# Gate loads a tile ahead, latents written back over their own tile, and two sets of transposes emitted later, in a one-core hybrid encoder layer

## The chip, the core and the metric

The kernel runs on one core of a Trainium2 chip. The metric is the device time of one execution in microseconds (us); below, "the time" is the median of several runs. The engines are TensorE (PE, matmuls and transposes; its weight loads are shown as PEld), VectorE (DVE), ScalarE (ACT), GpSimd (POOL) and SyncE (SP), which issues most of the DMA transfers from its queue.

## The reference

One layer is computed for 1024 new frames of one stream (the prompt) and 64 frames of a running stream (the sample, with 512 cached frames); together 1088 tokens of width 1024.

- Both streams are normalised, scaled and shifted by a conditioning vector, and projected once: `proj = h @ w_in`.
- Group A is latent attention. `latent_new = rms_norm(c_kv, g_kv_lora)` (256 wide) is an output and also the source of keys and values: `kv = (latent @ w_ukv)`, 4 heads of 128 + 128; a rotary part of 64 is appended to each key, the key is RMS-normalised per head and rotated. Attention is block-causal in chunks of 64.
- Group B is a gated linear recurrence, 4 heads with a state of 64x128: `o, s_new = gla_recurrence(q, k, v, log_a, s0)`, then `rms_norm(o, g_gla_out) * silu(r)`, where `r` is a part of the projection.
- The two groups are concatenated, projected by `w_out`, gated and added to the input; a squared-ReLU MLP of width 4096 follows.

All is in float32. The kernel computes each product of two float32 operands as three passes over split operands (high x high, high x low, low x high).

## The kernel before

Tokens are held in nine tiles of 128 (the ninth, tile 8, has the 64 frames of the sample); some products run over three chunks of 384, 384 and 320 tokens. `mm3` (L91 to L95) issues the three matmuls of one product, so most PE time stands under the lines L93, L94 and L95.

The program is emitted by several generators at once. `interleave` (L46) is a small planner: each generator yields (PE time it has just emitted in ns, a waiting time in ns, a condition), and the planner always takes the first generator in its list that is due, and adds its PE time to a clock. If none is due, the clock jumps. So the numbers in the `yield` lines are costs and due times by which instructions are put in program order; they are no waits on the chip. On the chip each engine runs its instructions in one order, and waits where an operand or a buffer isn't there. The order on an engine is not in all places the order of the program: a scheduler puts an instruction ahead of earlier ones when it takes it for ready sooner.

The kernel has these stages; the change touches the second to the fourth.

1. To some 95 us: normalisation, the first projection columns.
2. About 95 to 275 us: `interleave([weights, gla(), main(), gates(), lats])`. `gla` (L655) is the recurrence, a tile at a time, with a hierarchy of 7 levels of halves (6 for the tile of 64), each level a pair of matmuls (L747) between ACT and DVE work (`prep`, L671; masked copies, L755). After the last level the output `o` of the tile is multiplied out (L790, L794), squared on ACT (L799), scaled on POOL and DVE (L802, into `og`), and a closure `tail` (L805) is kept: it transposes `og` on PE (L808), copies the result with the gain on ACT into `mog` (L811) and stores it to `mix_d` in DRAM (L812). That closure is called in the next tile, after level 3 (L784). `main` (L573) runs the projections of values and gates meanwhile and stores the swish input to `r_d` (L618).
3. `gates` (L820) starts when all of `r_d` and `mix_d` has been emitted. For each of the nine tiles it loads `r` (L825) and the recurrence's output `mx` (L826) into two tiles of a ring of four buffers called `gv`, yields 1000, applies Silu on ACT (L829), multiplies on DVE (L830) and stores (L831). Beside it `latents` (L620) computes the compressed latents: 24 matmuls (`rows`, L265, into a bank `mm`), the sum of squares on ACT (L628), the root on POOL (L120, L121), the scaling on DVE into `cn` (L630, two buffers), an output (L634, L637). One tile later its transposes follow (L644: two on PE into a bank `tp`, of which there are two), two copies on ACT into a tile `cl` of one buffer (L647) and a store to `lat_d` (L648).
4. About 300 to 400 us: `interleave([weights, past_keys(), lats, query_main(), query_latents()])`, and then to about 610 us the attention stage with `keys_stream`, `queries_stream` and three `worker`s. The keys and values of a tile are made in `keys_values` (L876), for the cached frames (`past_keys`, L1056, whose latents are transposed at L1066) and for the new ones (`new_keys`, L1078): two groups of 12 matmuls of 512 columns with copies to `kn` and sums of squares on ACT (L900), a root on POOL (L904, L905), two multiplications on DVE (L907 into `kn`, L908 into `krt`), then a yield of 4500, four transposes of `kn` on PE (L914) and, 800 later, four of `krt` (L921). `query_main` (L1221) is the other PE work of this stage: nine blocks of 24 matmuls.
5. From 610 us to the end: output projection and MLP.

The pools of stage 2 and 3 (`gw`, which holds `gv`, and others) are closed after `gates`, and the pools of stage 4 (`kw` of the keys, `qp` of the query columns) are opened in that memory; a new tile there waits for the last use of the old tile in its place.

Of the kernel before, what the change touches and what calls it, by code (L numbers as in the profile page):

```python
# [10 lines left out]
F32 = mybir.dt.float32  # L11
# [3 lines left out]
ALU = mybir.AluOpType  # L15
# [4 lines left out]
P = 128  # L20
# [10 lines left out]
TILES = [(i * P, P) for i in range(8)] + [(SEQ, DEC)]  # L31
# [40 lines left out]
def layer(ctx: ExitStack, tc: tile.TileContext, I, O):  # L72
    nc = tc.nc
    ACT, DVE, POOL, PE, SP = nc.scalar, nc.vector, nc.gpsimd, nc.tensor, nc.sync
# [10 lines left out]
    def tp_bank():  # L85
        return psT.tile([P, 512], F32, name="tp")

    def g_bank():
        return psG.tile([P, 512], F32, name="g")
# [7 lines left out]
    def heads(ap):  # L97
        return ap.rearrange("p (h t) -> p h t", h=H)
# [123 lines left out]
    def has(*keys):  # L222
        return lambda: all(k in done or k in groups for k in keys)
# [3 lines left out]
    dp = hctx.enter_context(tc.tile_pool(reuse_waits="tile", name="dp", bufs=2, side="right"))  # L227
# [37 lines left out]
    def rows(key, off, n, w):  # L265

        wh, wl = groups[key]
        ps = mm_bank()
        for kt in range(KT):
            mm3(ps[:n, :w], h["h"][:, kt, off:off + n], h["l"][:, kt, off:off + n], wh[:, kt, :w], wl[:, kt, :w],  # L270
                kt == 0, kt == KT - 1)
            yield w * 1.25, 0, None
        return ps[:n, :w]
# [261 lines left out]
    with gctx:  # L535
# [84 lines left out]
        def latents():  # L620
            yield 2000, 0, has("D1")
            for i in (8, 0, 1, 2, 3, 4, 5, 6, 7):
                off, n = TILES[i]
                s = i == 8
                ps = yield from rows("D1", off, n, 320)
                cn_ = dp.tile([P, 256], F32, name="cn")
                s2 = dp.tile([P, 2], F32, name="s2")
                ACT.activation(cn_[:n], ps[:, 0:256], AF.Square, accum_out=s2[:n, 0:1])  # L628
                rstd(s2[:n, 1:2], s2[:n, 0:1], n, 1, 1.0 / 256)
                DVE.tensor_scalar(out=cn_[:n], in0=ps[:, 0:256], scalar1=s2[:n, 1:2], scalar2=None, op0=ALU.mult)  # L630
                ki = 12 if s else i
                ACT.copy(kraw[:n, ki], ps[:, 256:320])
                lat = dp.tile([P, 256], F32, name="lat", bufs=1)
                DVE.tensor_tensor(out=lat[:n], in0=cn_[:n], in1=gkv_bc[:n], op=ALU.mult)  # L634
                ol, ok = (O["lat_s"], O["kr_s"]) if s else (O["lat_p"], O["kr_p"])
                oo = 0 if s else off
                ACT.dma_start(ol[oo:oo + n], lat[:n])  # L637
                SP.dma_start(ok[oo:oo + n], kraw[:n, ki])
                tails.append((i, off, n, cn_))
                while len(tails) > (0 if i == 7 else 1):  # L640
                    j, o2, n2, c2 = tails.pop(0)
                    tp = tp_bank()
                    for b in range(2):
                        PE.transpose(tp[:, b * P:b * P + n2], c2[:n2, b * P:(b + 1) * P], ident[:n2, :n2])  # L644
                    cl = dp.tile([P, 2, P], F32, name="cl", bufs=1)
                    for b in range(2):
                        ACT.activation(cl[:, b, :n2], tp[:, b * P:b * P + n2], AF.Copy, scale=gkvT[:, b:b + 1])  # L647
                    SP.dma_start(lat_d[:, :, o2:o2 + n2], cl[:, :, :n2])  # L648
                    done.add(f"lat {j}")
                    yield 220, 1500, None  # L650
            done.add("end D1")
# [3 lines left out]
        def gla():  # L655
            rot = 0
            tail = None
# [54 lines left out]
            for i, (off, n) in enumerate(TILES):  # L712
# [23 lines left out]
                for lv, hf in enumerate(halves):  # L736
                    (kl, ql), nb = ready.pop(0), n // (2 * hf)
                    if lv + 2 < len(halves):
                        ready.append(prep(halves[lv + 2]))
                    elif begun is None:  # L740
                        if i + 1 < len(TILES) and f"gates {i + 1}" in done:
                            begun = begin(i + 1)
                    else:
                        begun[5].append(begun[2](begun[4][1]))
                    sc = g_bank()[:, 0:2 * P].rearrange("p (c j t) -> p c j t", c=2, j=2)
                    for p in range(2):
                        PE.matmul(sc[:n, p, :, :n // 2], lhsT=kl[:, n * p:n * p + n], rhs=ql[:, :, p, :n // 2],  # L747
                                  start=True, stop=True)
                    sc = sc[:n, :, :, :n // 2].rearrange("p c j (b h) -> p (c j) b h", h=hf)
                    to = ST[:n, :, :n].rearrange("p c (b r h) -> p r c b h", r=2, h=hf)[:, 1]  # L750
                    if nb == 1:
                        ACT.copy(to[:hf], sc[:hf])
                    else:
                        mlv = 6 - (hf.bit_length() - 1)
                        DVE.copy_predicated(to, masks[:n, mlv, :n // 2].rearrange("p (o b h) -> p o b h", o=1, h=hf)  # L755
                                            .broadcast_to([n, H, nb, hf]), sc)
                    yield 440, 1800, None
                    if lv == 0:
                        tp = tp_bank()
                        for p in range(2):  # L760
                            PE.transpose(tp[:n, P * p:P * p + P], kk[:, p, :n], ident)
                        kt_ = gw.tile([P, 256], F32, name="kt_", bufs=1)
                        ACT.copy(kt_[:n], tp[:n, 0:256])
                    if lv == 2:
                        sp = g_bank()
                        for p in range(2):
                            PE.matmul(sp[:, 256 * p:256 * p + 256], lhsT=kt_[:n, P * p:P * p + P],
                                      rhs=gv[:n, 256 * p:256 * p + 256], start=True, stop=True)
                        for p in range(2):
                            for j in range(2):  # L770
                                ps, cs = slice(64 * j, 64 * j + 64), slice(P * j, P * j + P)
                                src = sp[ps, 256 * p + P * j:256 * p + P * j + P]
                                if i == 0:
                                    ACT.copy(sb_new[ps, p, cs], src)
                                else:
                                    DVE.scalar_tensor_tensor(out=sb_new[ps, p, cs], in0=sb_old[ps, p, cs],
                                                             scalar=E1[ps, p, n - 1:n], in1=src,
                                                             op0=ALU.mult, op1=ALU.add)
                        if i >= 7:
                            dst = O["st_s"] if smp else O["st_p"]  # L780
                            for p in range(2):
                                for j in range(2):
                                    SP.dma_start(dst[2 * p + j], sb_new[64 * j:64 * j + 64, p, P * j:P * j + P])
                    if lv == 3 and tail is not None:  # L784
                        tail()
                        tail = None
                o = mm_bank()
# [10 lines left out]
                for hd in range(H):  # L798
# [4 lines left out]
                                  in1=s4[:n, 4:8].rearrange("p (h t) -> p h t", t=1).broadcast_to([n, H, P]), op=ALU.mult)  # L803
# [16 lines left out]
        def gates():  # L820

            yield 0, 2000, has("end C1", "gla out")
            for i, (off, n) in enumerate(TILES):
                r, mx = (gw.tile([P, 512], F32, name="gv", bufs=4) for _ in range(2))
                SP.dma_start(heads(r)[:, :, :n], r_d[:, :, off:off + n])  # L825
                SP.dma_start(heads(mx)[:, :, :n], mix_d[:, 4:8, off:off + n])  # L826
                yield 0, 1000, None
                r, mx = (heads(t)[:, :, :n] for t in (r, mx))
                ACT.activation(r, r, AF.Silu)  # L829
                (DVE if i % 2 else DVE).tensor_tensor(out=r, in0=r, in1=mx, op=ALU.mult)  # L830
                SP.dma_start(mix_d[:, 4:8, off:off + n], r)  # L831

        lats = Stream(latents())
# [42 lines left out]
    def keys_values(lh, ll, ki, tab, n, kv, slot):  # L876
# [11 lines left out]
                          in1=t_[:n, :, 32:64].broadcast_to([n, 2, 32]), op=ALU.subtract)  # L888
        DVE.tensor_tensor(out=R[:n, 0, :, 32:64], in0=a[:n, :, 32:64].broadcast_to([n, 2, 32]),
                          in1=t_[:n, :, 0:32].broadcast_to([n, 2, 32]), op=ALU.add)  # L890
        kr = kw.tile([P, H, P], F32, name="krt", bufs=1)
        for g in range(2):
# [6 lines left out]
            for j in range(2):  # L899
# [8 lines left out]
        DVE.tensor_tensor(out=kr[:n], in0=R[:n].rearrange("p t d c -> p t (d c)").broadcast_to([n, H, P]),  # L908
                           in1=rs, op=ALU.mult)
        cs = slice(P * slot, P * slot + n)  # L910
        yield 0, 4500, None
        tp = heads(tp_bank())
        for hd in range(H):
            PE.transpose(tp[:, hd, :n], kn[:n, hd], ident[:n, :n])  # L914
# [959 lines left out]
```

## Time and profile before

| what | value |
|---|---|
| median of 3 runs | 1394.36 us (1393.22 to 1397.86) |
| time of the profiled execution | 1394.88 us |
| span of the profiled execution | 1393.1 us |
| PE busy in the span | 1340.9 us (96%) |
| DVE, ACT, POOL busy | 900.3, 685.3, 63.6 us |
| PE not busy, 95 to 275 us | 12.85 us |
| PE not busy, 275 to 400 us | 10.85 us |
| PE not busy, 400 to 525 us | 3.21 us |

The span runs from the first to the last instruction in the trace; the time of the execution is 1.8 us longer. PE is busy nearly throughout, so what is to be had lies in the stretches where it isn't, and in those where its granted clock is below 1.00. A row of a waiting view says who waited, "<-" for what, the sum in us, how often and the longest. In a row of a timeline stand the start, the duration, the engine, the line, the operation, output<-inputs, and in brackets the engine's idle time just before with what ended it.

### The profile page before, as it was taken

The page shows a single profiled execution, that of the slowest core. Times are in us where ns is not written, and L with a number is a line of the kernel's source. Part 1 is how long each engine was busy: PE and PEld are TensorE (multiplying, and loading weights), DVE is VectorE, ACT ScalarE, POOL GpSimd, SP SyncE. Part 2 cuts the span into 40 slices and gives each one's busy share as a digit, 9 for nine tenths or more (in the row PEclk, how much of TensorE's full clock was granted, in tenths as well). Part 3 has the DMA queues.
Part 4 walks back from the last instruction along what each step waited for, and adds up shares of the span by engine and source line. Part 5 has one row for each costly group of instructions (what it writes and reads, how often), then busy time and mean ns, then how long its engine had stood idle before and what let it go on. Part 6 is the DMA issues. An engine that isn't in the chain of part 4 may idle for free.

```text
span 1393.1 us, 26171 instructions
## 1 busy us (share of the span) xinstructions
PE 1340.9 (96%) x10014; PEld 1261.0 (91%) x10014; DVE 900.3 (65%) x2040; ACT 685.3 (49%) x1756; POOL 63.6 (5%) x115
## 2 busy tenths in 40 slices
PE   6998899988999999999999999999999999999998
PEld 5897789887876778899998999999999999999998
DVE  5688788337465766656789756566555866874554
ACT  5467667435345566653475544544444343343342
POOL 0010000011010210000000000000000000000000
PEclk9999999999999999999999999999999999999999
DMA  9320012384253442164225444444248764543440
GB/s 346 121 73 9 16 54 76 115 241 120 90 163 113 149 133 61 52 200 137 80 79 177 160 150 151 129 154 145 100 176 289 276 218 154 185 127 95 125 129 33
DMA packets 165591, 188.14 MB, mean 135 GB/s; under 512 B 16814, under 2 KB 116442, under 8 KB 165466
## 3 DMA queue, kind: packets, MB, share of 16 engines
q1 hardware_dynamic: 158010, 180.90, 40.5%
q10 hardware_dynamic: 7456, 5.57, 1.2%
q8 instruction: 79, 1.29, 0.4%
q14 instruction: 46, 0.38, 0.1%
HBM read 132.97 MB, written 53.46 MB: 134 GB/s over the span
## 4 chain that ended last, share of the span: by engine, by line
PE 82%; DVE 6%; ACT 4%; DMA 4%; issue 1%; POOL 1%; SPq 1%; DVEq 0%; ACTq 0%; POOLq 0%
PE mm L93 14%; PE mm L95 14%; PE mm L94 13%; PE g L93 6%; PE g L95 6%; PE g L94 6%; PE mm L992 3%; PE tp L93 3%; PE tp L95 3%; PE tp L94 3%; PE g L1019 3%; PE mm L166 2%; DMA raw<-in_w_in 1%; PE tp L1029 1%; PE g L747 1%
## 5 line engine op out<-in xcount | busy, mean ns | idle before, releaser
L101 ACT CAST opers<-quad 128x512 fp32r<-128x512 f32 x112 | 69.5, 620 | 184.5 <-PE mm L95 145.8
L102 DVE TENSOR_TENSOR opers<-quad,opers 128x512 fp32r<-128x512 f32 x112 | 77.2, 690 | 114.5 <-ACT opers L101 114.5
L95 PE MATMUL mm<-opers 128*128 128x272 f32 x448 | 128.9, 288 | 0.0
L93 PE MATMUL mm<-opers 128*128 128x272 f32 x448 | 128.5, 287 | 0.3 <-DVE e L1806 0.3
L94 PE MATMUL mm<-opers 128*128 128x272 f32 x448 | 128.3, 286 | 0.0
L93 PE MATMUL mm<-ah,wh 128*128 128x272 f32 x424 | 122.5, 290 | 3.4 <-ACT wh L101 2.2
L94 PE MATMUL mm<-al,wh 128*128 128x272 f32 x424 | 121.9, 288 | 0.0
L95 PE MATMUL mm<-ah,wl 128*128 128x272 f32 x424 | 121.8, 289 | 0.0
L93 PE MATMUL mm<-hh,wh 128*128 128x384 f32 (+2 forms) x264 | 90.7, 347 | 1.9 <-ACT hh L101 1.9
L95 PE MATMUL mm<-hh,wl 128*128 128x384 f32 (+2 forms) x264 | 87.5, 332 | 0.0
L94 PE MATMUL mm<-hl,wh 128*128 128x384 f32 (+2 forms) x264 | 87.4, 332 | 0.0
L93 PEld LDWEIGHTS mm<-opers 128*128 128x128 f32 x448 | 84.6, 189 | 0.5 <-issue 0.5
L95 PEld LDWEIGHTS mm<-opers 128*128 128x128 f32 x448 | 84.3, 188 | 0.0
L93 PEld LDWEIGHTS mm<-ah,wh 128*128 128x128 f32 x424 | 80.3, 189 | 4.2 <-ACT wh L101 2.6
L94 PEld LDWEIGHTS mm<-opers 128*128 128x128 f32 x448 | 84.0, 188 | 0.0
L94 PEld LDWEIGHTS mm<-al,wh 128*128 128x128 f32 x424 | 80.1, 189 | 0.0
L95 PEld LDWEIGHTS mm<-ah,wl 128*128 128x128 f32 x424 | 79.9, 189 | 0.0
L102 DVE TENSOR_TENSOR opers<-ru,opers 128x544 fp32r<-128x544 f32 x108 | 77.6, 719 | 2.2 <-ACT opers L101 2.0
L101 ACT CAST opers<-ru 128x544 fp32r<-128x544 f32 x108 | 69.4, 643 | 13.1 <-PE mm L95 11.7
L101 ACT CAST wh<-ru 128x512 fp32r<-128x512 f32 x67 | 41.3, 618 | 67.6 <-PE g L94 24.5
L102 DVE TENSOR_TENSOR wl<-ru,wh 128x512 fp32r<-128x512 f32 x67 | 45.9, 689 | 36.3 <-ACT wh L101 36.0
L93 PE MATMUL mm<-wh,hh 128*128 128x264 f32 (+3 forms) x216 | 66.4, 309 | 0.5 <-ACT gv L583 0.3
(409 smaller groups left out, 4310.4 us busy)
## 6 DMA issues: line engine op xcount, KB each, us to landing
ru<-u_d SPq DMA_DIRECT2D x108, 272.0 KB, 2.7
raw<-in_w_ada SPq DMA_DIRECT2D x40, 512.0 KB, 3.9
ru<-in_w_up SPq DMA_DIRECT2D x32, 512.0 KB, 4.1
quad<-in_w_down SPq DMA_DIRECT2D x16, 1024.0 KB, 6.6
u_d<-st SPq DMA_DIRECT2D x60, 272.0 KB, 2.1
u_d<-sc SPq DMA_DIRECT2D x45, 272.0 KB, 2.2
raw<-in_w_in SPq DMA_DIRECT2D x22, 256.0 KB, 4.2
x<-in_xo_T SPq DMA_DIRECT2D x8, 544.0 KB, 5.0
```

The source lines that it names most:

```text
L93: PE.matmul(out, lhsT=ah, rhs=bh, start=first, stop=False, skip_group_check=more)
L94: PE.matmul(out, lhsT=ah, rhs=bl, start=False, stop=False, skip_group_check=more)
L95: PE.matmul(out, lhsT=al, rhs=bh, start=False, stop=last, skip_group_check=more)
L101: ACT.copy(hi, src)
L102: eng.tensor_tensor(out=lo, in0=src, in1=f32(hi), op=ALU.subtract)
L166: mm = PE.matmul(acc[32 * j:32 * j + 32, 0:256], lhsT=scT[:, k, :], rhs=was[k][:, 256 * j:256 * (j + 1)], start=(k == 0), stop=(k == KT - ...
L747: PE.matmul(sc[:n, p, :, :n // 2], lhsT=kl[:, n * p:n * p + n], rhs=ql[:, :, p, :n // 2], start=True, stop=True)
L992: PE.matmul(sp[:n, :w], lhsT=x[:, hd, :n], rhs=y[:, hd, :w], start=(j == 0), stop=(j == 4))
L1019: PE.matmul(op[:n, 0:P], lhsT=pt[:kw, k, :n], rhs=kvs[kt // 4].v[:kw, kt % 4, hd], start=(kt == 0), stop=(kt == nkt - 1))
L1029: PE.transpose(tp[:kw, k, :n], pr[k0 // 4][:n, P * k:P * k + kw], ident[:n, :n])
```

## The change

Five places are edited.

- `gates`: the two loads of tile i + 1 are written ahead of the computation of tile i, with the first tile's loads ahead of the loop; the yield before each computation goes from 1000 to 2500. The ring of four `gv` buffers stays.
- `latents`: `cn` has three buffers instead of two, and the separate tile `cl` is gone: the ACT copies of the transposed latents go back into the tile `cn` they came from, and the store to `lat_d` reads it there.
- `gla`: the closure `tail` of the tile before is called after level 5 instead of after level 3.
- `keys_values`: the yield before the transposes of `kn` goes from 4500 to 6500.
- A choice between DVE and DVE in `gates` is written as DVE.

```
-                cn_ = dp.tile([P, 256], F32, name="cn")
+                cn_ = dp.tile([P, 256], F32, name="cn", bufs=3)
...
-                    cl = dp.tile([P, 2, P], F32, name="cl", bufs=1)
+
+                    cl = c2.rearrange("p (b t) -> p b t", b=2)
...
-                    if lv == 3 and tail is not None:
+                    if lv == 5 and tail is not None:
...
-            for i, (off, n) in enumerate(TILES):
+            tiles = {}
+
+            def load(i):
+                off, n = TILES[i]
                 r, mx = (gw.tile([P, 512], F32, name="gv", bufs=4) for _ in range(2))
                 SP.dma_start(heads(r)[:, :, :n], r_d[:, :, off:off + n])
                 SP.dma_start(heads(mx)[:, :, :n], mix_d[:, 4:8, off:off + n])
-                yield 0, 1000, None
-                r, mx = (heads(t)[:, :, :n] for t in (r, mx))
+                tiles[i] = [heads(t)[:, :, :n] for t in (r, mx)]
+
+            load(0)
+            for i, (off, n) in enumerate(TILES):
+                if i + 1 < len(TILES):
+                    load(i + 1)
+                yield 0, 2500, None
+                r, mx = tiles.pop(i)
                 ACT.activation(r, r, AF.Silu)
-                (DVE if i % 2 else DVE).tensor_tensor(out=r, in0=r, in1=mx, op=ALU.mult)
+                DVE.tensor_tensor(out=r, in0=r, in1=mx, op=ALU.mult)
                 SP.dma_start(mix_d[:, 4:8, off:off + n], r)
...
-        yield 0, 4500, None
+        yield 0, 6500, None
```

## The prediction

> **What bounds the kernel now.** I read the page first, then busy time by stretches, then the waits of PE, then the timelines of PE, ACT and SP around each wait.
>
> ```profile
> PE 1340.9 (96%) x10014; PEld 1261.0 (91%) x10014; DVE 900.3 (65%) x2040; ACT 685.3 (49%) x1756; POOL 63.6 (5%) x115
> ```
>
> ```profile
> 95.00:275.00 180.00, 167.15 (x1102) 150.71 (x1102) 130.78 (x401) 115.10 (x428) 12.37 (x21) 0.96 0.17 52
> 275.00:400.00 125.00, 114.15 (x712) 102.64 (x711) 62.06 (x152) 47.89 (x166) 16.27 (x30) 0.99 0.52 150
> ```
>
> PE sets the time. The columns of the second fence are the stretch, its length, busy time of PE, PEld, DVE, ACT and POOL, the granted clock, the DMA share and GB/s. PE is idle for 180 - 167.15 = 12.85 us while the recurrence runs, and for 125 - 114.15 = 10.85 us in the stretch of gates, latents and first keys. The change removes no matmul and no transpose, so all it can give is idle time, and clock lost after idle time, in these stretches and the start of attention. Which waits could go, by the waits of PE from 95 to 610 us:
>
> ```profile
> PE tp L914 <- DVE kn L907: 6.9, 6, 1.7
> PE tp L644 <- ACT cl L647: 4.5, 2, 3.7
> ...
> PE tp L808 <- DVE og L802: 1.8, 2, 1.0
> ```
>
> These are the three sets of transposes that the change touches: 13.2 us together, 0.9% of the time.
>
> **Latents and gate loads.** On PE, in its timeline:
>
> ```profile
> 286.57 0.34 PE L644 MATMUL tp<-ident,cn 64*128 64x64 f32 x2 [0.19 <-DVE cn L630]
> 289.61 0.38 PE L1066 MATMUL tp<-ident,past 128*128 128x128 f32 x2
> 291.65 0.44 PE L644 MATMUL tp<-ident,cn 128*128 128x128 f32 x2 [0.79 <-ACT cl L647]
> 299.93 0.33 PE L644 MATMUL tp<-ident,cn 128*128 128x128 f32 x1 [3.71 <-ACT cl L647]
> ```
>
> The tiles come in the order 8, 0, 1, 2 and so on. There are two banks `tp`. The transposes of the cached latents (L1066) took one of them at 289.61, and their reader on ACT (L1072) ran only at 312.62 (row below). So tile 1's transposes at 299.93 needed the bank of tile 0, and waited for tile 0's copies on ACT:
>
> ```profile
> 291.09 0.50 ACT L647 ACTIVATE cl<-tp,vT 128x64 f32<-128x64 f32 x2
> ...
> 298.74 0.63 ACT L829 ACTIVATE gv<-gv 128x512 f32<-128x512 f32 x1 [2.74 <-DMA gv<-r_d]
> 299.27 0.61 ACT L647 ACTIVATE cl<-tp,vT 128x128 f32<-128x128 f32 x2
> 299.77 0.38 ACT L628 ACTIVATE cn<-mm 128x256 f32<-128x256 f32 x1
> ```
>
> They stood behind a Silu that waited 2.74 us for its load; and `cl`, one buffer, was still being stored for tile 8, by an issue that began at 294.75:
>
> ```profile
> 277.90 0.56 SPq L825 DMA_DIRECT2D gv<-r_d  x1
> ...
> 281.96 0.36 SPq L831 DMA_DIRECT2D mix_d<-gv  x1
> ```
>
> ```profile
> 294.75 1.34 SPq L648 DMA_DIRECT2D lat_d<-cl  x1
> ```
>
> The idle time cost clock as well (columns as above):
>
> ```profile
> 295.00:300.00 5.00, 1.29 (x10) 1.03 (x9) 1.12 (x2) 2.00 (x6) 0.00 (x0) 1.00 0.85 246
> 300.00:305.00 5.00, 5.00 (x25) 5.00 (x26) 1.60 (x3) 1.12 (x5) 1.21 (x2) 0.66 1.01 269
> 330.00:335.00 5.00, 3.36 (x26) 3.04 (x25) 3.32 (x8) 1.83 (x5) 1.33 (x2) 1.00 0.11 33
> 435.00:440.00 5.00, 3.87 (x35) 2.69 (x33) 3.22 (x14) 2.32 (x11) 1.34 (x2) 1.00 0.56 157
> 440.00:445.00 5.00, 4.98 (x25) 3.54 (x25) 2.64 (x9) 3.09 (x11) 0.00 (x0) 0.66 0.21 80
> ```
>
> A clock of 0.66 from 300 to 305 loses (1 - 0.66) x 5 = 1.7 us. So up to 4.5 + 1.7 = 6.2 us lie here.
>
> What the edits do to it. The load ahead itself I cost at nothing: the load for the second tile was issued at 277.90, before the first store at 281.96, though the program writes it after; the machine order has it ahead already, and the ring is still of four buffers. What counts is the due time. By the planner's arithmetic, each of the nine gate tiles took 1000 rounded up to PE steps of 400, so at a clock of 10,520 they were all emitted, and with them the 8 steps each of tiles 8 and 0, their 220 + 1500, and six steps of tile 1; there the next stage began with L1066. The rows agree: L1066 stands between the transposes of tiles 8 and 0. With 2500 the ninth comes at 24,080, after tiles 8, 0, 1, 2, 3 and three steps of tile 4. L1066 moves behind the transposes of tile 2; those of tile 1 find the bank of tile 8, free since its copies on ACT (291.09 + 0.50). The 3.71 us goes.
>
> What is late next: `cn` now stays occupied until its store has landed, and with three buffers tile 2 reuses that of tile 8.
>
> ```profile
> lat_d<-cl SPq DMA_DIRECT2D x1, 64.0 KB, 4.2
> ```
>
> ```profile
> 301.66 0.48 DVE L630 TENSOR_SCALAR cn<-mm,s 128x256 f32<-128x256 f32 x1 [0.71 <-POOL s L121]
> ```
>
> That store, issued as now at 294.75, lands at 294.75 + 4.2 = 298.95. The chain from the square on ACT (299.77) to the end of the scaling (301.66 + 0.48) takes 2.4 us, so tile 2's transposes are ready at 301.3. PE gets there earlier:
>
> ```profile
> 279.19 0.31 PE L93 MATMUL mm<-wh,hh 128*64 128x320 f32 x1
> ```
>
> Two tiles took from 279.19 to 286.38 (286.57 less 0.19 idle), 3.6 us each; five tiles and three pairs of transposes of 0.44 end at 279.19 + 18.0 + 1.3 = 298.5. So 301.3 - 298.5 = 2.8 us may come back. ACT holds behind that waiting square only copies and Silus, which PE needs a tile later. I take 6.2 - 2.8 = 3.4 us as the gain, between 6.2 and a loss (first rival).
>
> The Trainium skill, "TensorE: Matmul & The Clock Gate", Part 1, says that the clock halves after an idle window of some 3.4 us and recovers after a busy one. The stretch at 300 us agrees, behind a wait of 3.71 us; that at 440 us does not, where 5 - 3.87 = 1.13 us idle came before. By the rule, the shorter waits of the keys carry no loss of clock, and the sum would be 7.7 us as below.
>
> By the rows, 1.64 us idle from 330 to 335 was followed by no drop that my stretches show, and 1.13 us from 435 to 440 by a loss of (1 - 0.66) x 5 = 1.7 us. So clock after short waits is worth 0 to 1.7 us; I take 0, since the idle time before 440 is not a wait of the touched lines, and keep 1.7 for the low end.
>
> **Keys.** The waits of L914 in PE's timeline:
>
> ```profile
> 321.99 0.66 PE L914 MATMUL tp<-ident,kn 128*128 128x128 f32 x4 [0.95 <-DVE kn L907]
> 322.69 0.63 PE L921 MATMUL tp<-ident,krt 128*128 128x128 f32 x4
> 332.29 0.63 PE L914 MATMUL tp<-ident,kn 128*128 128x128 f32 x4 [1.64 <-DVE kn L907]
> 344.13 0.63 PE L914 MATMUL tp<-ident,kn 128*128 128x128 f32 x4 [1.67 <-DVE kn L907]
> 354.49 0.66 PE L914 MATMUL tp<-ident,kn 128*128 128x128 f32 x4 [1.01 <-DVE kn L907]
> ```
>
> With two at 426 and 500 us they make the 6.9 us. Each wait is shorter than the 2 us added, so where the machine order follows the program's, it goes whole. It does not follow it everywhere: L921 comes 0.70 us after L914 began, with none of the 800 between them. There the order is by expected readiness, because the keys begin late: their pools lie where the gates' buffers were.
>
> ```profile
> 312.62 0.38 ACT L1072 CAST lath<-tp 128x256 fp32r<-128x256 f32 x1 [0.93 <-DMA mix_d<-gv]
> ```
>
> By then PE has run ahead of the planner, the places of the first one or two key tiles are past, and 2000 more changes nothing for them. I take half, 3.5 of 6.9. Bounds: 0 and 6.9. It delays each key tile by up to 2 us; five tiles, 10 us. The cover is `query_main`: the last L914 that waits in this stage is at 354.49, and from 375 to 400 PE is busy throughout with other products. Without that cover it would cost 10 us.
>
> ```profile
> 375.00:400.00 25.00, 25.00 (x174) 22.12 (x173) 8.65 (x26) 5.42 (x22) 1.34 (x2) 1.00 0.40 119
> ```
>
> **The tail of the recurrence.** Two waits of L808 sum to 1.8 us, one of them 1.0:
>
> ```profile
> 161.93 0.66 PE L808 MATMUL tp<-ident,og 128*128 128x128 f32 x4 [1.02 <-DVE og L802]
> ```
>
> After 162 us PE has little other work, so time won there is lost again at the next level; the other 0.8 us I count. Below: the copies into `mog` (four on ACT) now come just ahead of the next tile's squares.
>
> ```profile
> L811 ACT ACTIVATE mog<-tp,vT x36: 307/362/378, 128.4 to 274.1; 128x128 f32<-128x128 f32 x32, 128x64 f32<-128x64 f32 x4
> ```
>
> Four of 0.36 us are 1.4 us per tile; if they stood in the chain in the three or four tiles before 200 us, 5 us. Bounds: -1.8 and +5.
>
> **Sum.** 3.4 + 3.5 + 0.8 = 7.7 us: 1394.88 - 7.7 = 1387.2 on the profiled execution's own time, which is 0.5 above the median, so 1386.7 us.
>
> **Rivals.** *Slower: the gates end after PE's other work.* Keys and query columns cannot start before them.
>
> ```profile
> L825 SPq DMA_DIRECT2D gv<-r_d x9: 530/542/823, 275.3 to 307.9; - x9
> ...
> L830 DVE TENSOR_TENSOR gv<-gv x9: 426/692/693, 281.2 to 313.3; 128x512 f32<-128x512 f32 x8, 128x256 f32<-128x256 f32 x1
> L831 SPq DMA_DIRECT2D mix_d<-gv x9: 360/360/625, 282.0 to 313.8; - x9
> ```
>
> ```profile
> 315.32 0.40 PE L93 MATMUL g<-wh,lath 128*128 128x512 f32 x1
> ```
>
> They took 313.8 - 275.3 = 38.5 us, 4.3 per tile. After the change PE is through the latents at 279.2 + 9 x 3.6 + 8 x 0.44 + 2.8 = 317.9. If a lower place in the order makes a gate tile 1.5 us slower, the gates end at 327.3: 9.4 us of idle PE, 1.5 until the first product of the keys (315.3 now, against 313.8), and 1.7 of clock, 12.6 in all; 1394.4 - 7.7 + 12.6 = 1399.3 us. It decides from about 0.3 us per tile (313.8 + 2.7 + 1.5 = 318.0) and turns the sign from about 1.0. For it: the DMA share is 0.85 to 1.01 from 295 to 305. Against it: the ring sets the pace, and it is the same ring. Two tiles per turn:
>
> ```profile
> gv<-r_d SPq DMA_DIRECT2D x8, 256.0 KB, 4.0
> ...
> mix_d<-gv SPq DMA_DIRECT2D x8, 256.0 KB, 3.1
> ```
>
> 4.0 + 0.63 (Silu) + 0.69 (multiplication) + 3.1 = 8.4 us, 4.2 per tile, nearly what was measured. Chance 0.10.
>
> *Nothing moves.* If the order is by readiness in all three places, L914 and L808 stay, and the 2.8 us come back with a second such wait: 1394.4 - (6.2 - 2 x 2.8) = 1393.8 us. For it: 277.90 against 281.96, and L921. Against it: L1066 stands where the planner put it. Chance 0.22.
>
> *The `mog` copies in the chain*: 1394.4 - 7.7 + 0.8 + 5 = 1392.5 us. Chance 0.06.
>
> **How the numbers follow.** Forecast 1386.7 us, chance 0.62, own range 1381 to 1390. About 0.3% (4.2 us) is what a measurement can tell from no change, so faster is under 1390.2 and slower over 1398.5. Low end: all bounds at best are 6.2 + 6.9 + 1.8 + 1.7 = 16.6 us, 1377.8; I take 1380, since all at once is unlikely. High end 1397: it holds the second and third rival and the milder half of the first. Faster 0.62; same 0.27 (second and third rival, 0.22 + 0.03, and a gate delay of about 1 us, 0.02); slower 0.11 (0.08 of the first rival, 0.03 of the third with clock lost as well).
>
> **What would show it.** Right: no wait of L644 for ACT copies near 3.7 us and clock 1.00 from 295 to 305; L1066 first after 297 us; waits of L914 halved; one wait of L808 left; the last gate store near 314. Wrong: PE idle between 315 and 330 with keys waiting for gate stores; waits on ACT squares (L628) for stores to `lat_d` of several us; the same six waits of L914; new waits at L747 between 100 and 200 us.

## The result

| kernel | median | runs | ratio to before, 95% interval |
|---|---|---|---|
| before | 1394.73 us | 1392.66 to 1397.86 (11) | |
| after | 1399.87 us | 1398.61 to 1402.40 (11) | 1.0036 [1.0028, 1.0044] |

The change makes the kernel slower by 0.36%, 5.1 us. The profiled execution of after took 1398.64 us, its span is 1396.9 us, 3.8 us longer than before's. PE's busy time, on the page and in two stretches (columns as in the prediction's second fence):

```profile
PE 1346.7 (96%) x10014; PEld 1262.2 (90%) x10014; DVE 900.8 (64%) x2040; ACT 685.5 (49%) x1756; POOL 64.1 (5%) x115
```

```profile
95.00:275.00 180.00, 168.69 (x1112) 152.67 (x1112) 130.64 (x401) 115.52 (x429) 12.04 (x21) 0.96 0.18 52
275.00:400.00 125.00, 117.33 (x728) 103.63 (x726) 66.93 (x162) 49.68 (x171) 17.13 (x32) 0.99 0.55 160
...
575.00:600.00 25.00, 20.24 (x126) 17.37 (x125) 16.93 (x36) 16.61 (x34) 0.00 (x0) 0.93 0.57 160
```

Where the prediction expected its gain, PE is less idle than before: 11.31 us instead of 12.85 from 95 to 275 us, and 7.67 instead of 10.85 from 275 to 400 us. The last row is a stretch that the prediction left out. There PE is idle for 4.76 us at a clock of 0.93; before:

```profile
575.00:600.00 25.00, 23.70 (x166) 21.25 (x165) 22.00 (x55) 19.75 (x42) 0.53 (x1) 1.00 0.46 130
```

Three rows of PE's timeline cut the span into stages: the last transposes of the recurrence, the last sums of the query columns, the last transposes of each attention tile. Before, then after. (The lines of before from L645 to L820 have a number 1 higher in after, those from L829 on 10 higher.)

```profile
273.02 0.46 PE L808 MATMUL tp<-ident,og 64*128 64x64 f32 x4
390.66 0.83 PE L1228 MATMUL g<-ones,sq 128*128 128x1 f32 x6
593.45 0.60 PE L1133 MATMUL tp<-ident,mo 128*128 128x128 f32 x4
606.87 0.60 PE L1133 MATMUL tp<-ident,mo 128*128 128x128 f32 x4
```

```profile
271.28 0.46 PE L809 MATMUL tp<-ident,og 64*128 64x64 f32 x4
385.29 0.83 PE L1238 MATMUL g<-ones,sq 128*128 128x1 f32 x6
586.39 0.55 PE L1143 MATMUL tp<-ident,mo 128*128 128x128 f32 x3 [2.29 <-ACT mo L1054]
609.87 0.60 PE L1143 MATMUL tp<-ident,mo 128*128 128x128 f32 x4
```

At the end of the query columns the change is 391.49 - 386.12 = 5.4 us ahead. From there to the end of attention it takes 610.47 - 386.12 = 224.4 us, before 607.47 - 391.49 = 216.0: 8.4 us are lost, so it leaves attention 3.0 us late. The last tile comes 23.5 us after the one before it, where before it came 13.4 after: 10.1 us more. The loss shows in this distance; the experiments below show that not all of it is made there.

The waits of PE in after, from 95 to 610 us:

```profile
PE tp L1039 <- ACT prob L1013: 3.9, 3, 2.5
PE tp L924 <- DVE kn L917: 3.8, 5, 1.0
PE tp L644 <- DVE cn L630: 3.3, 1, 3.3
...
PE tp L1143 <- ACT mo L1054: 2.3, 1, 2.3
...
PE tp L809 <- DVE og L803: 1.0, 1, 1.0
```

The three waits that the change aimed at are smaller (L924 was 6.9 us, L644 4.5, L809 1.8). Of the waits for ACT at the end of attention, that of L1143 is new and that of L1039 longer (2.3 us before). What stood ahead of them, in ACT's timeline of after:

```profile
582.64 1.04 ACT L1173 CAST wh<-raw 128x1024 fp32r<-128x1024 f32 x1 [2.19 <-DMA raw<-in_w_out]
583.59 0.36 ACT L1054 ACTIVATE mo<-g,sta 128x128 f32<-128x128 f32 x1
585.03 1.04 ACT L1173 CAST wh<-raw 128x1024 fp32r<-128x1024 f32 x1 [1.07 <-DMA raw<-in_w_out]
585.98 0.36 ACT L1054 ACTIVATE mo<-g,sta 128x128 f32<-128x128 f32 x1
586.24 0.86 ACT L101 CAST mh<-raw 128x816 fp32r<-128x816 f32 x1
...
588.50 0.78 ACT L1013 ACTIVATE prob<-mm,sta,ssq 128x512 f32<-128x512 f32 x1 [0.91 <-DVE sta L1009]
```

These casts belong to `wo_loader` (L1156 in after), another generator of the attention stage. Once all queries are projected (and a generator `mods` is through), it loads five blocks of `w_out` (three at once, the next when one is used), casts them on ACT, subtracts on DVE (L105), and yields 1000 and 1500 between blocks; the casts are kept in program order. The output copies of the last tile but one (L1054) stand behind casts that wait 2.19 and 1.07 us for loads, and PE waits for those copies. The last tile has 1024 keys, so each of its heads has two exponentials of 512; its first one runs at 588.50, 202.4 us after the query columns. Before it ran at 585.53, 194.0 us after them, and between the casts, in ACT's timeline:

```profile
585.53 0.78 ACT L1003 ACTIVATE prob<-mm,sta,ssq 128x512 f32<-128x512 f32 x1 [1.47 <-DVE sta L999]
...
587.05 0.61 ACT L1163 CAST wh<-raw 128x512 fp32r<-128x512 f32 x1
587.56 0.37 ACT L1044 ACTIVATE mo<-g,sta 128x128 f32<-128x128 f32 x1
587.82 1.04 ACT L1163 CAST wh<-raw 128x1024 fp32r<-128x1024 f32 x1
...
589.77 1.05 ACT L1163 CAST wh<-raw 128x1024 fp32r<-128x1024 f32 x1 [0.42 <-DMA raw<-in_w_out]
590.73 0.77 ACT L1003 ACTIVATE prob<-mm,sta,ssq 128x512 f32<-128x512 f32 x1
```

### The profile page after: what moved, and what is told of

Same layout as the page of the kernel before. It is cut to its first block, busy times and chain, and to the rows that moved or that the text cites. A ratio compares the mean times of both kernels' runs of the same rounds, so it can differ in the third digit from the quotient of the medians.

```text
span 1396.9 us, 26163 instructions
## 1 busy us (share of the span) xinstructions
PE 1346.7 (96%) x10014; PEld 1262.2 (90%) x10014; DVE 900.8 (64%) x2040; ACT 685.5 (49%) x1756; POOL 64.1 (5%) x115
## 4 chain that ended last, share of the span: by engine, by line
PE 80%; DVE 9%; ACT 4%; DMA 3%; issue 2%; POOL 1%; SPq 0%; ACTq 0%; DVEq 0%; POOLq 0%
PE mm L93 14%; PE mm L95 13%; PE mm L94 13%; PE g L93 5%; PE g L95 5%; PE g L94 5%; PE tp L93 3%; PE tp L95 3%; PE tp L94 3%; PE mm L1002 3%; PE g L1029 2%; PE mm L166 2%; PE g L748 2%; DMA raw<-in_w_in 1%; PE tp L1039 1%
## 5 line engine op out<-in xcount | busy, mean ns | idle before, releaser
L101 ACT CAST opers<-quad 128x512 fp32r<-128x512 f32 x112 | 69.4, 620 | 184.6 <-PE mm L95 145.7
L101 ACT CAST opers<-ru 128x544 fp32r<-128x544 f32 x108 | 69.4, 643 | 13.1 <-PE mm L95 11.7
L101 ACT CAST wh<-ru 128x512 fp32r<-128x512 f32 x67 | 41.3, 618 | 67.6 <-PE g L94 24.5
```

The costliest lines, as they stand in the source:

```text
L101: ACT.copy(hi, src)
```

## The experiments

**Which part.** First the parts one by one. The keys alone (kernel before), then all but the keys (changed kernel):

```
-        yield 0, 4500, None
+        yield 0, 6500, None
```

> The kernel before with one part of the change alone: the transposes of the keys due 6500 instead of 4500 after their copies. Theory K (the later due time of the keys reorders what the planner emits during attention, so that the casts of w_out wait for their loads in front of the last tile's softmax): the waits of the key transposes fall by about 3 us, but attention up to 610 us takes some 8 us longer, so slower than before by 3 to 6 us, 1398 to 1401 us, with a gap of 4 us or more on PE ahead of the last attention tile near 585 us. Theory G (the gates' edit, which moves the end of that stage, reorders attention): only the gain of the key waits is left, 1391 to 1393 us. Theory S (attention's end is sensitive to any small shift; no part is the cause by itself): anything from 1389 to 1402 us, decided by where the casts of w_out fall among the exponentials of the last tile.

```
-        yield 0, 6500, None
+        yield 0, 4500, None
```

> The changed kernel with the keys' due time back at 4500, all else kept. Theory K: the gain up to the end of the query columns without the 3 us of the keys is left and the loss in attention is gone: 1391 to 1394 us. Theory G: the loss in attention stays, and the key waits are back: 1400 to 1404 us. Theory S: between 1389 and 1404 us, with the loss where the casts of w_out stand in front of the last tile's exponentials, and none where they stand apart.

Measured: 1402.12 us, 1.0051 [1.0038, 1.0063], for the keys alone; 1390.54 us, 0.9966 [0.9952, 0.9980], for the rest. Both signs are theory K's, though the times lie just outside its ranges (1.1 us above, 0.5 us below), and theory G, which had the signs the other way round, falls: one number turns a gain of 0.34% into a loss of 0.36%. The keys alone have the gap (4.83 us idle from 575 to 600 us); by stretches, all-but-the-keys has none there (columns as above):

```profile
575.00:600.00 25.00, 25.00 (x190) 23.40 (x189) 18.76 (x45) 18.19 (x37) 0.00 (x0) 1.00 0.70 204
```

The gates' edit alone (with the loads a tile ahead), and the latents' alone (with three buffers `cn`):

```
-                yield 0, 1000, None
+                yield 0, 2500, None
```

> The kernel before with the gates' edit alone (loads a tile ahead, due 2500). Theory K: the 3.7 us wait of the latents' transposes for ACT goes, some of it comes back, no loss in attention: 1391 to 1395 us. Theory G: the loss in attention is here: 1398 to 1402 us, with a gap of 4 us or more on PE near 585 us. Theory S: 1389 to 1402 us, by the place of the casts.

```
-                    cl = dp.tile([P, 2, P], F32, name="cl", bufs=1)
+                    cl = c2.rearrange("p (b t) -> p b t", b=2)
```

> The kernel before with the latents copied back into their own place alone (three buffers cn, no tile cl). Theories K and G: 1393.5 to 1396 us, no change that can be told from none, because the wait of the third latent tile for ACT at 300 us stays behind the Silus. Theory S: 1390 to 1400 us, by what the shifted emission does to attention.

Measured: gates 1393.60 us, 0.9989 [0.9980, 0.9999]; latents 1396.73 us, 1.0017 [1.0007, 1.0027]. The gates' time lies in theory K's range and speaks against theory G once more. The latents' edit alone loses a little, which theories K and G did not have (0.7 us above their range; theory S allowed for it); among its waits of PE a new one stands at the first product of the cached keys:

```profile
PE g L93 <- ACT lath L1072: 3.8, 1, 3.8
```

Gates and latents together, without the recurrence's edit (`lv == 3` kept):

> The kernel before with the gates' and the latents' edits, and neither the keys' nor the recurrence's. If the last edit (the output's transposes two levels later) brings the 0.8 us that the prediction gave it: 1391 to 1392 us, 0.8 above the kernel with all but the keys. If it brings nothing, 1390.5; if it brings most of what that kernel gains beyond the gates alone: 1392.5 to 1394 us.

Measured: 1391.90 us, 0.9984 [0.9974, 0.9994]. That is in the range expected if the recurrence's edit brings its 0.8 us, but the 1.4 us to all-but-the-keys can't be told from nothing, since the intervals overlap. Against the median of before beside them the two edits gave -1.5 and +1.7 us alone and -3.1 together. By the ratios, together is little better than the gates alone (0.9984 against 0.9989, the intervals overlap); what shows is that the latents' edit, which loses alone, does not lose beside the gates'.

**Which keys.** In after, 6500 for the cached keys and the ninth tile only, and the reverse:

```
+        yield 0, 6500 if kv in (kvS[0], kvN[0]) else 4500, None
```

> The changed kernel with the keys' transposes due 6500 only for the cached keys and the ninth tile (the four and one tiles emitted before attention), and 4500 for the keys that are made during attention. If the loss comes from the keys made during attention (theory A), the early gain stays and attention is as in the kernel with all keys at 4500: 1390.5 less up to 3 us, so 1387 to 1390 us. If any later key in front of attention is enough to shift what is emitted there (theory B): 1396 to 1401 us.

> The reverse: 4500 for the cached keys and the ninth tile, 6500 for the keys that are made during attention. Theory A: the loss is all here, 1399 to 1404 us, with PE idle for 4 us or more in the stretch from 575 to 600 us. Theory B: 1390 to 1394 us.

Measured: 1392.64 us, 0.9983 [0.9973, 0.9993], and 1399.34 us, 1.0032 [1.0022, 1.0042]. The second is in theory A's range; the first is 2.6 us above theory A's and well under theory B's, with PE idle for 0.12 us from 575 to 600 us. So the loss comes with the keys made during attention. The early keys show no gain either: 1392.64 is above the 1390.54 without them, though the intervals overlap.

**Chain or order.** Two explanations remained: the chain of a key tile is longer, so that the last tiles start late; or the planner, with other due times, emits the end of attention in another order. The chain was shortened in the changed kernel (all keys 6500) by loading the latents of the next key tile ahead:

```
-        lraw = get_T(kw, lat_d, 2, off, n, "latr")
-        yield 0, 1875, None
+        lraw = ahead.pop(i, None)
+        if lraw is None:
+            lraw = get_T(kw, lat_d, 2, off, n, "latr")
+            yield 0, 1875, None
+        if i + 1 < 8:
+            ahead[i + 1] = get_T(kw, lat_d, 2, *TILES[i + 1], "latr")
```

> The changed kernel (all keys due 6500) with the latents of the next key tile loaded a tile ahead in attention, which takes the wait of 1875 out of the chain of each key tile, so that the chain of a tile is as long in due times as it was with 4500. In the program's order the last casts of w_out stand as in the changed kernel. Theory P (the longer chain of the key tiles, 17.1 us a tile instead of 14.5, lets the last tiles start late, and attention ends without cover): the chain is back near 14.5 to 15 us a tile and the time at 1391 to 1395 us. Theory O: the order is the same at the end, so 1397 to 1401 us.

Measured: 1400.34 us, 1.0044 [1.0029, 1.0058]. The first seven key tiles now come at 393.5 to 479.4 us, 14.3 apart (after: 17.0), and the loss stays. Theory P falls. Half the delay for all keys:

```
-        yield 0, 6500, None
+        yield 0, 5500, None
```

> The changed kernel with all keys' transposes due 5500, half way between 4500 and 6500. In the program's order the casts of w_out and the exponentials of the last tile then stand as they do with 4500. Theory O (the order at the end of attention decides, not how late the keys are): as fast as with 4500, 1388 to 1392 us, with less than 1 us idle on PE from 575 to 600 us. Theory L (every us by which the keys come later lengthens attention): half the loss, 1394 to 1396 us.

Measured: 1394.60 us, 1.0002 [0.9990, 1.0014]: in time as theory L had it, but without the gap (1.23 us idle from 575 to 600, as before's 1.30, at clock 1.00; last tile 13.3 us after the one before). So a longer due time costs time even without the gap, and the gap is a second term. The next pair was chosen to part them: 6500 for the first four tiles of attention alone, and for the last four alone.

```
+        yield 0, 6500 if kvs and kv is kvs[0] else 4500, None
```

> The changed kernel with 6500 for the keys of the first four tiles of attention alone, 4500 for all others. The order at the end of attention is the one of 4500, with the last tile's first exponentials between the casts of w_out. Theory O (the order at the end decides): no gap near 585 us, PE idle under 1.5 us from 575 to 600 us at a clock of 1.00, last tile 13 to 14 us after the one before it, 1390 to 1394 us. Theory L (lateness itself): half of the loss or more, 1394 to 1398 us, without that gap.

```
+        yield 0, 6500 if kvs[1:] and kv is kvs[1] else 4500, None
```

> The changed kernel with 6500 for the keys of the last four tiles alone, 4500 for all others. In the program's order all casts of w_out stand ahead of the last tile's first exponentials. Theory O: the gap near 585 us is back, 3 us or more idle on PE from 575 to 600 us, last tile 18 us or more after the one before it, 1396 to 1401 us. Theory L: 1394 to 1398 us, half of the loss, with no such gap.

Measured: 1393.86 us, 0.9992 [0.9982, 1.0001], and 1398.02 us, 1.0023 [1.0014, 1.0033]. The gap is where theory O had it: none in the first (1.24 us idle from 575 to 600, clock 1.00), 3.01 us idle in the second. The times do not decide: 1393.86 is 0.1 us from theory L's range and 3.3 above all-but-the-keys, and the profiled run of the second lost 3.4 us to the clock near 440 us, far ahead of the gap (stretch of 50 us, (1 - 0.93) x 50):

```profile
400.00:450.00 50.00, 47.97 (x311) 32.90 (x309) 30.62 (x101) 25.85 (x98) 5.31 (x8) 0.93 0.38 117
```

ACT at the end of attention, first four, then last four:

```profile
583.51 0.78 ACT L1013 ACTIVATE prob<-mm,sta,ssq 128x512 f32<-128x512 f32 x1 [1.47 <-DVE sta L1009]
...
585.04 0.61 ACT L1173 CAST wh<-raw 128x512 fp32r<-128x512 f32 x1
585.55 0.37 ACT L1054 ACTIVATE mo<-g,sta 128x128 f32<-128x128 f32 x1
585.81 1.04 ACT L1173 CAST wh<-raw 128x1024 fp32r<-128x1024 f32 x1
```

```profile
586.71 1.04 ACT L1173 CAST wh<-raw 128x1024 fp32r<-128x1024 f32 x1
588.04 0.58 ACT L1145 COPY mt<-tp 128x512 f32<-128x512 f32 x1 [0.29 <-PE tp L1143]
...
589.06 1.04 ACT L1173 CAST wh<-raw 128x1024 fp32r<-128x1024 f32 x1 [0.44 <-ACT mt L1145]
590.09 0.78 ACT L1013 ACTIVATE prob<-mm,sta,ssq 128x512 f32<-128x512 f32 x1
```

In the second the casts do not wait for loads, yet the gap is there. In the rows of DVE and of PE:

```profile
587.19 0.16 DVE L1009 SCALAR_TENSOR_TENSOR sta<-sta,ssq 128x1 f32<-128x1 f32 x1
```

```profile
591.01 0.66 PE L1039 MATMUL tp<-ident,prob 128*128 128x128 f32 x4 [3.01 <-ACT prob L1013]
```

By the order of the rows, DVE had the maxima for the exponential of 590.09 ready at 587.35; it then stood on ACT behind the rest of a cast, a copy and one more cast, and PE waited 3.0 us for it. So this gap comes from the order on ACT, where the last tile's first softmax stands behind all the casts; in after the casts' waits for loads add to it.

**The casts.** One number more in the changed kernel, to spread the casts; and, in the good order of 4500, casts pushed together by hand:

```
             done.add(f"wo {m}")
-            yield 1000, 1500, None
+            yield 1000, 3500, None
```

> The changed kernel (all keys due 6500) with one number more changed: a cast of w_out is due 3500 instead of 1500 after the one before it, so that in ACT's order the exponentials of the last tile's first heads stand between the casts. Theory W (the casts of w_out, waiting for their loads, hold up the copies and exponentials behind them on ACT, and their subtractions those on DVE): the idle time of PE near 585 us falls from 4.8 us to below 2, the clock stays at 1.00, 1392 to 1396 us. Theory F (attention with later keys ends with too little other work to cover its waits, whatever the casts do): 1398 to 1402 us.

```
             done.add(f"wo {m}")
-            yield 1000, 1500, None
+            yield 0, 0, None
```

> The changed kernel with the keys' due time back at 4500, and a cast of w_out due at once after the one before it: the collision is put in by hand where the order was a good one. Theory W: a gap of 2 us or more on PE behind the casts opens between 580 and 600 us, and the time rises from 1390.5 to 1393 to 1398 us. Theory F: within 1.5 us of 1390.5.

Measured: spread casts 1396.91 us, 1.0012 [1.0001, 1.0023], so 0.0024 of the 0.0036 is won back; the wait of L1143 is gone and the last tile's first exponential comes 195.8 us after the query columns. The time is between the two theories, 0.9 us above theory W's range, and W's other signs are missed as well: PE is idle for 2.32 us from 575 to 600 at a clock of 0.93, since the casts of the mixed outputs (L101, from `out_early`) now stand ahead of the last exponentials and wait in their turn. Its timelines of ACT and PE:

```profile
592.21 0.88 ACT L101 CAST mh<-raw 128x816 fp32r<-128x816 f32 x1 [1.32 <-DMA raw<-mix_d]
594.38 0.37 ACT L1054 ACTIVATE mo<-g,sta 128x128 f32<-128x128 f32 x1 [1.29 <-PE g L1029]
```

```profile
596.67 1.12 PE L1039 MATMUL tp<-ident,prob 128*128 128x128 f32 x4 [2.32 <-ACT prob L1013]
```

Bunched casts: 1392.97 us, 0.9984 [0.9976, 0.9993]; 2.4 above the kernel it was made from, with overlapping intervals, 1.49 us idle from 575 to 600, and a clock of 0.97 from 400 to 450, ahead of the casts. Neither theory has it: the gap that theory W asked for did not open, and the time is above theory F's. In this run the last tile's first exponential still stands ahead of the last two casts, so the order of after was not made by hand, and the run does not show whether that order alone is enough.

**The wait at 300 us.** In after, the transposes of latent tile 2 (of the order 8, 0, 1, 2) wait 3.3 us:

```profile
299.69 0.69 PE L644 MATMUL tp<-ident,cn 128*128 128x128 f32 x2 [3.30 <-DVE cn L630]
```

Gates due 6000 with keys at 4500:

```
-                yield 0, 2500, None
+                yield 0, 6000, None
```

> The changed kernel with the keys' due time at 4500 and the gates' at 6000 instead of 2500. Theory Q (the wait of the third latent tile, 3.3 us at 300 us, comes from its Square standing on ACT behind a Silu that waits for its gate's load): the Silus find their loads landed, the wait falls below 1.5 us, and the query columns end 2 to 4 us earlier, 1387 to 1389.5 us. Theory B (the wait comes from the buffer cn, which is held until its store has landed, as the prediction had it): the wait stays near 3 us, 1390 to 1392 us.

Measured: 1398.52 us, 1.0032 [1.0019, 1.0044]. Neither theory: the Silus still wait (up to 3.6 us), as the ring of four buffers, two for each tile, lets a load go only after the store of the tile two before it, and the cached latents' transposes moved behind all of the latents (to 319.55 us). So that run does not part Q from B. The trace of after says more (timelines of ACT and of SP's queue, then the DMA view with KB and us from issue to landing):

```profile
294.42 0.63 ACT L839 ACTIVATE gv<-gv 128x512 f32<-128x512 f32 x1 [1.81 <-DMA gv<-r_d]
...
297.22 0.63 ACT L839 ACTIVATE gv<-gv 128x512 f32<-128x512 f32 x1 [2.17 <-DMA gv<-r_d]
297.75 0.37 ACT L628 ACTIVATE cn<-mm 128x256 f32<-128x256 f32 x1
```

```profile
289.60 0.57 SPq L649 DMA_DIRECT2D lat_d<-cn  x1
```

```profile
lat_d<-cn SPq DMA_DIRECT2D x6, 128.0 KB, 2.9
lat_d<-cn SPq DMA_DIRECT2D x1, 64.0 KB, 3.9
```

The store of tile 8, which frees the buffer `cn`, was issued at 289.60 and had landed by 293.5 with the 3.9 us of its row. The Square (L628) came at 297.75 all the same, directly behind two Silus that had waited for their loads. So the rows speak for theory Q; no run took the Silus out of the way.

**All kernels in one table**: us from the recurrence's end to that of the query columns, from there to the end of attention, what of that the clock lost, from the end of the query columns to the last tile's first exponential, and the last tile's distance to the one before. Each is worked out from the rows of the lines named above in the kernel's own trace; the clock's part is (1 - clock) x 5, summed over stretches of 5 us.

| kernel | keys in attention | median | to query end | attention | lost to the clock | first exponential | last tile |
|---|---|---|---|---|---|---|---|
| before | 4500 | 1394.7 | 118.0 | 216.0 | 1.7 | 194.0 | 13.4 |
| gates only | 4500 | 1393.6 | 116.6 | 214.7 | 0 | 192.9 | 13.3 |
| latents only | 4500 | 1396.7 | 120.1 | 214.6 | 0 | 192.8 | 13.3 |
| gates and latents | 4500 | 1391.9 | 114.3 | 217.4 | 3.4 | 195.5 | 13.3 |
| all but keys | 4500 | 1390.5 | 115.2 | 214.6 | 0 | 192.8 | 13.3 |
| early keys only | 4500 | 1392.6 | 116.6 | 215.2 | 0 | 193.3 | 13.3 |
| gates due 6000 | 4500 | 1398.5 | 120.5 | 217.6 | 3.4 | 195.7 | 13.3 |
| bunched casts | 4500 | 1393.0 | 114.7 | 218.9 | 1.7 | 195.5 | 13.9 |
| 5500 | 5500 | 1394.6 | 117.6 | 217.9 | 0 | 196.2 | 13.3 |
| first four | 6500 / 4500 | 1393.9 | 115.0 | 218.6 | 0 | 196.8 | 13.3 |
| spread casts | 6500 | 1396.9 | 115.8 | 220.5 | 1.7 | 195.8 | 19.4 |
| last four | 4500 / 6500 | 1398.0 | 115.0 | 223.8 | 3.4 | 203.0 | 22.8 |
| after | 6500 | 1399.9 | 114.4 | 224.4 | 1.7 | 202.4 | 23.5 |
| load ahead | 6500 | 1400.3 | 115.5 | 225.2 | 3.4 | 203.0 | 23.4 |
| keys in attention | 6500 | 1399.3 | 114.5 | 225.7 | 3.4 | 203.3 | 24.0 |
| keys alone | 6500 | 1402.1 | 116.3 | 225.8 | 3.4 | 202.5 | 24.8 |

Every kernel with a first exponential past 200 us has an attention of 224 us or more (rounded) and a last tile 22.8 us or more behind the one before; every one with less has neither. Theory S falls with it: seven kernels change other parts, or nothing, and leave the keys of attention and the casts as before, and none of them has the gap.

Without the clock's part, these seven take 214.0 to 215.2 us for attention, 5500 takes 217.9, the first four 218.6, the last four 220.4, and the four at the bottom of the table 221.8 to 222.7. An estimate from these single profiles: of the 9.8 us by which the attention of after is longer than that of all-but-the-keys, some 4 us come without any gap, as in the first four, some 4 with the gap, and 1.7 are clock.

What stays open is the part without a gap: the first-four and 5500 kernels lose 3 to 4 us in attention against all-but-the-keys at a clock of 1.00. Counted from start to start on PE, that time lies in small pieces, and not in the same ones: for the first four 2.2 us more around the three-pass products of keys and queries, 1.6 around the matmuls of L166, 1.1 around L1039; for 5500 it is 2.9 around L1002. That the keys come later is not enough as a reason: with the load ahead the seventh key tile comes at 479.4 us and in all-but-the-keys at 479.6, yet without the clock's part its attention takes 7.2 us more. Which interleaving does it was not tried.

## Why the prediction was wrong

The forecast was 1386.7 us, range 1380 to 1397; measured 1399.9, on the other side and outside.

- **The step that failed** is the keys' term: "It delays each key tile by up to 2 us; five tiles, 10 us. The cover is `query_main`". It counted the five key tiles ahead of attention and named their cover. The eight tiles made during attention issue from the same line; the prediction counted the waits at 426 and 500 us among its gain and put no cost against what else would be emitted in those 2 us. That is the loss: a gain of 3.5 us was forecast for the keys, and alone they cost 7 us (1402.12 against 1395.07); the two runs that part the keys put the loss with those made during attention. Moving a due time is not moving one step: the order of other work in the stage moved with it, here of the casts and the last tile's softmax. What that order does on ACT is shown for the gap; for the 3 to 4 us that come without a gap the cause is open. None of the rivals named a mechanism after 330 us.
- **Waits of keys.** L924 fell from 6.9 to 3.8 us, 3.1 against 3.5 forecast, but that match is luck. With the keys back at 4500 and all else changed the same waits are 4.8 us, so the due time took 1.0 of the 3.1 and the other edits 2.1 (alone, in the kernel before, it took 2.3):

```profile
PE tp L924 <- DVE kn L917: 4.8, 5, 1.3
```

Nor did a wait shorter than the 2 us added go whole: the four waits between 320 and 360 us are still there in after, 0.7 to 1.0 us each. And what went is worth nothing as time: with the early keys alone delayed the kernel is not faster than with none.
- **Latents and gates**, 3.4 us forecast: for the two edits alone 3.1 us by the medians and 2.2 by the ratio (0.9984), so the size was about right. Within it the path was partly as told: L644 no longer waits for ACT's copies (L647), L1076 comes at 302.55, behind tile 2's transposes, as the planner's arithmetic said. What comes back, at tile 2 as forecast, was put at 2.8 us and is 3.3, with the clock loss too, by stretches of after:

```profile
295.00:300.00 5.00, 1.70 (x12) 1.43 (x11) 1.51 (x3) 1.77 (x7) 0.73 (x2) 0.91 0.92 255
300.00:305.00 5.00, 5.00 (x29) 4.98 (x28) 2.21 (x5) 1.72 (x6) 0.74 (x2) 0.75 0.96 262
```

(0.09 + 0.25) x 5 = 1.7 us, the same as before. The cause named, `cn` held by its store, is not what the rows show: that store was not issued "as now at 294.75" but at 289.60, and two Silus with late loads stood ahead of the Square. So the near match of 2.8 and 3.3 is luck too. And "The load ahead itself I cost at nothing" was nearly fair: the nine Silus of that stage still wait for 13.2 us in all, 16.3 before.
- **The tail**, 0.8 us: one of two waits of L808 went, as said, but the recurrence ends at 271.3 us without that edit (gates and latents) and at 271.4 with it (all but the keys). No gain shows, and as the kernels with that edit end it anywhere from 270.2 to 272.1 us, 0.8 could not be told from nothing.
- **The gates-late rival** was wrong: the pace stayed, and the first product of the keys comes at 313.52 (315.32 before). **The `mog` rival** did not come: the recurrence ends at 271.7 us, 273.5 before.

## What to carry over

In a kernel ordered by a planner with costs and due times, the price of a longer due time is not only the wait it removes: list all generators that run while it counts, up to the end of the last stage in which the line is used, and compare the resulting order of each engine there. At the end of a stage, where one tile is left, see whether its first softmax is emitted ahead of preparatory work for the next stage; here it came behind it, and PE stood idle for 3 to 5 us. A change of several edits should be timed edit by edit: here three of them are worth 0.34% (1390.54 us, 0.9966 [0.9952, 0.9980], the best version found), and one number takes it away and as much again.

## What the runs showed of the hardware

The granted clock halved after little idle time. In the kernel with gates and latents alone, PE was idle for 1.15 us from 430 to 435 us (stretches; the clock is the third column from the right):

```profile
430.00:435.00 5.00, 3.85 (x34) 2.78 (x34) 2.99 (x14) 2.81 (x11) 1.02 (x1) 0.97 0.69 212
435.00:440.00 5.00, 5.00 (x21) 3.29 (x21) 2.33 (x7) 2.15 (x8) 0.00 (x0) 0.50 0.05 20
440.00:445.00 5.00, 5.00 (x29) 3.41 (x29) 0.94 (x5) 1.70 (x6) 0.00 (x0) 0.85 0.36 108
```

(0.03 + 0.50 + 0.15) x 5 = 3.4 us lost, 2.8 of which show in its attention (217.4 us against 214.6 of all-but-the-keys, with the same due times of the keys). The Trainium skill, "TensorE: Matmul & The Clock Gate", Part 1, gives an idle window of some 3.4 us as what sets the clock back; this stretch does not agree, and neither did the one at 440 us before. In after at 440 us the clock stayed at 1.00. So a difference of 2 to 3 us between two single profiles can be one such event, and the comparisons here go by medians, by several kernels of one order, or with the clock's part set apart.
